# SwiGLU products read back near their use, a lag of three turns, and a ring of eight weight units

## Chip, core and metric

One core of one Trainium2 chip runs the kernel. The metric is the device time of one execution in microseconds (us), lower is better; of several runs the median counts.

## What is computed

A decoder trunk of four layers on 256 tokens of width 1024, all in float32. Each layer is half a SwiGLU feed-forward block, a mixer, and half a second feed-forward block, each behind an RMSNorm and added to x. The mixers of the four layers are a short gated convolution, multi-head latent attention (16 heads, causal), a spatial gating block, and the convolution again.

```python
# x: (1, 256, 1024); D_FF 2816; four layers
def swiglu(x, w_gate, w_up, w_down):
    return (jax.nn.silu(x @ w_gate) * (x @ w_up)) @ w_down
...
    for i in range(DEPTH):
        x = x + 0.5 * swiglu(rms_norm(x, norm_g[i, 0]), ffn_gate[i, 0], ffn_up[i, 0], ffn_down[i, 0])
        hn = rms_norm(x, norm_g[i, 1])
        kind = i % N_MIXERS
        ...
        x = x + mix
        x = x + 0.5 * swiglu(rms_norm(x, norm_g[i, 2]), ffn_gate[i, 1], ffn_up[i, 1], ffn_down[i, 1])
```

The convolution mixer is (b * conv(c * h)) @ w_out with b, c, h parts of x @ w_in. The attention mixer projects to a 416-wide vector (w_a), from it to keys, values (w_ukv) and queries (w_uq), normalises and rotates them, and ends with w_o.

## The kernel before

**Two tiles, one list of weights.** The 256 tokens are two tiles of 128. Each weight matrix is cut into units of 128 x 1024 elements (512 KB), in a fixed order. A unit is loaded from DRAM into one of six raw buffers (`Weights.load`, L93, on SP's queue), split into a high part by ScalarE (`make`, L106) and a low part by VectorE (`complete`, L113), both in a ring of N_UNITS buffers, and used once by tile 0 and once by tile 1. A product of two float32 numbers is three matmuls: high by high, high by low, low by high (`products`, L299, L300, L302). `get` makes units up to AHEAD (4) ahead of tile 0's current one, 3 while a tile is between blocks. The raw buffer of unit u is loaded again, with unit u+6, when the low part of u is written.

**Turns.** Each tile is a Python generator (`stream`); what it issues from one `yield` to the next is a turn, most often one unit, six matmuls of 512 columns. The program is written out by hand: tile 0 gets LAG turns alone (L1004), and then the two take turns, tile 1 first (L1006 to L1009). `later(n, f)` issues f after n turns, those of both tiles counted. All engines execute what is issued to them in that order, and semaphores alone hold them back.

**A feed-forward block.** After IDLE turns without matmuls come 44 turns of gate and up: chunks of 512 columns, where the first three (gate 0, up 0, gate 1) go in two halves of k (`linear_group`). Then 22 turns of down (`rows_into_x`): k-tiles 0 to 9 one by one with 1024 columns, and the last 12 (DOWN_TAIL) in pairs, once for each half of the columns. When a gate chunk is done ScalarE takes Silu of it (L479); when an up chunk is done VectorE makes the product (L487) and transposes it in blocks of 32 (L489) into a `big` buffer. Two chunks make a record (three of them: 8, 8 and 6 k-tiles of 128). `turned` (L269) writes the record to DRAM one turn later (L275), reads it back four turns after the product in four transfers that put the blocks in transposed place (L279), into a second `big`, and from turn 12 on takes it, four k-tiles at a time: ScalarE makes the high part (L285), VectorE the low part (L286), both in slots, of which there are 34. They are held until the down turns use them. There are four `big` buffers and four DRAM buffers for records.

**Around the blocks.** At a block's end x is updated in halves (`residual`, L398 and L400), squared for the norm (L381), and turned for the next block by TensorE (`turn_by_pe`, L261, L441, L253, L254) or through DRAM (L421, L425, L431). The convolution makes c * h (L548), turns it by TensorE three turns later (L261), applies the taps on VectorE (L528, L530) and gates it (L537). In the attention block the streams have turns without matmuls: four ahead of it (IDLE_MLA), three after the queries (Q_WAIT), three ahead of w_o (O_WAIT), and tile 0 has one after each of its four score turns (T0_PACE). L781 ends the rotation of keys and queries, L787 evicts the w_a product, L919 is the exponential, L930 copies the turned probabilities.

Of the kernel before, what the change touches and what calls it, by code (L numbers as in the profile page):

```python
# [24 lines left out]
P = 128  # L25
D = 1024
# [14 lines left out]
PER_RAW = 1  # L41
SMALL = 0
N_UNITS = 9
# [6 lines left out]
LAG = 4  # L50
# [3 lines left out]
SKEW = 2  # L54
# [10 lines left out]

class Weights:


    def __init__(self, nc, raw_pool, pool):
        self.nc, self.raw_pool, self.pool = nc, raw_pool, pool  # L70
        self.raws = []
        self.units = []
# [6 lines left out]
    def add(self, w, c0, width, n_kt, per_unit, k=0):  # L79

        v = w.rearrange("(kt p) n -> p kt n", p=P)
        while k < n_kt:
            n_rows = min(n_kt - k, per_unit * (1 if len(self.units) < SMALL else max(1, PER_RAW * UNIT // (per_unit * width))))
            for j in range(0, n_rows, per_unit):
                self.units.append((len(self.raws), j, min(per_unit, n_rows - j), width))
            self.raws.append((v[:, k : k + n_rows, c0 : c0 + width], n_rows, width))
            k += n_rows

    def load(self, upto):
        while len(self.loaded) < min(upto, len(self.raws)):  # L90
            view, n_rows, width = self.raws[len(self.loaded)]
            raw = self.raw_pool.tile([P, n_rows, width], F32, tag="raw", name=f"raw{len(self.loaded)}")
            self.nc.sync.dma_start(out=raw, in_=view)  # L93
            self.loaded.append(raw)

    def make(self):
        nc = self.nc
        u = len(self.made)
        if u == len(self.units):
            return  # L100
        r, j, n, width = self.units[u]
        self.load(r + 1)
        src = self.loaded[r][:, j : j + n, :]
        hi = self.pool.tile([P, n, width], F32R, tag="whi", name=f"whi{u}")
        lo = self.pool.tile([P, n, width], F32R, tag="wlo", name=f"wlo{u}")
        nc.scalar.activation(hi, src, AF.Copy)  # L106
        self.made.append((hi, lo, n))
        last = u + 1 == len(self.units) or self.units[u + 1][0] > r
        self.half_made.append((hi, lo, src, r + 1 + N_RAW if last else 0))
# [22 lines left out]
def trunk(ctx: ExitStack, tc: tile.TileContext, x, positions, norm_g, ffn_gate, ffn_up, ffn_down,  # L132
          conv_w_in, conv_k, conv_w_out, mla_w_a, mla_q_norm, mla_w_uq, mla_kv_norm, mla_w_ukv,
          mla_q_gain, mla_k_gain, mla_w_o, sg_w_in, sg_v_norm, sg_w_s, sg_b, sg_w_out, out):
    nc = tc.nc

# [7 lines left out]
    banks = ctx.enter_context(tc.tile_pool(name="banks", bufs=8, space=PSUM))  # L144

    ids = [0]
# [38 lines left out]
    W = Weights(nc, raw_pool, w_pool)  # L185
    cursor = [0] * NT
    in_chain = [False] * NT

    def unit(t):
        cursor[t] += 1  # L190
        return W.get(cursor[t] - 1, AHEAD if not any(in_chain) else CHAIN_AHEAD)
# [20 lines left out]
    def start():  # L212
# [7 lines left out]
        make_identity(nc, ident)  # L220
# [83 lines left out]
    def linear(t, a, width, n_kt):  # L304

        ps = acc()
        k = 0
        while k < n_kt:
            w = unit(t)
# [7 lines left out]
    def plan_rows(w, n_kt, tail):  # L317

        W.add(w, 0, D, n_kt - tail, 1)
        for h in range(2):  # L320
            W.add(w, 512 * h, 512, n_kt, 2, n_kt - tail)

    def rows_into_x(t, a, n_kt, tail, factor, then):
# [3 lines left out]
        for k in range(n_kt - tail):  # L327
            products(ps, a(k), k % 4, unit(t), 0, cols, k == 0, False)
            yield
        for h in range(2):  # L330
            for k in range(n_kt - tail, n_kt, 2):
                w = unit(t)
# [12 lines left out]

    def plan_group(parts, width, n_kt):

        for k in range(0, n_kt, n_kt // 2):
            for w, c0 in parts:
                W.add(w, c0, width, k + n_kt // 2, UNIT // width, k)  # L350

    def linear_group(t, a, width, n_kt, done):

        ps = [acc() for _ in done]
        for k0 in range(0, n_kt, n_kt // 2):
            for n in range(len(done)):
                k = k0
                while k < k0 + n_kt // 2:
                    w = unit(t)
                    for j in range(w[2]):  # L360
                        products([ps[n][:, :width]], a[(k + j) // 4], (k + j) % 4, w, j, [slice(0, width)], k + j == 0, k + j == n_kt - 1)
                    k += w[2]
                    if k == n_kt:
                        done[n](ps[n])
                    yield
# [95 lines left out]
    def plan_ffn(i, j):  # L461
        gate, up = ffn_gate[i, j], ffn_up[i, j]
        plan_group([(gate, 0), (up, 0), (gate, 512)], 512, NK)
        W.add(up, 512, 512, NK, 2)
        for c, w in FF_CHUNKS[2:]:
            for m in (gate, up):
                W.add(m, c, w, NK, UNIT // w)
        plan_rows(ffn_down[i, j], DFF // P, DOWN_TAIL)

    def ffn(t, i, j, _, then):  # L470
        a, r = yield from normed(t, IDLE_FIRST if i + j == 0 else (IDLE_DMA, IDLE_PE)[j])
        hs = []
        sg = [None] * len(FF_CHUNKS)
        z = []

# [5 lines left out]
        def up_done(n, ps):  # L481
# [10 lines left out]
            if z[1] == nk:  # L492
                turned(z[0], nk, hs)

        yield from linear_group(t, a, 512, NK, [lambda ps: gate_done(0, ps), lambda ps: up_done(0, ps), lambda ps: gate_done(1, ps)])
        for n, (c, w) in enumerate(FF_CHUNKS):
            if n > 1:
                gate_done(n, (yield from linear(t, a, w, NK)))
                yield
            if n > 0:  # L500
                up_done(n, (yield from linear(t, a, w, NK)))
                yield
        yield from rows_into_x(t, lambda k: hs[k // 4], DFF // P, DOWN_TAIL, 0.5, then)


    def plan_conv(ia):
        plan_group([(conv_w_in[ia], part * D) for part in (1, 2, 0)], 512, NK)
        for part in (1, 2, 0):
            W.add(conv_w_in[ia], part * D + 512, 512, NK, 2)
        plan_rows(conv_w_out[ia], NK, OUT_TAIL)  # L510

    def conv(t, i, ia, shared, then):
# [43 lines left out]
        yield from linear_group(t, a, 512, NK, [lambda ps, f=f: f(0, ps) for f in (c_done, h_done, b_done)])  # L556
        for f in (c_done, h_done, b_done):
            f(1, (yield from linear(t, a, 512, NK)))
# [477 lines left out]
```

## Time and profile before

| | |
|---|---|
| median of 3 runs | 1859.11 us (1858.88 to 1860.58) |
| the profiled execution | 1856.6 us, span 1854.9 us |
| granted TensorE clock, mean | 0.998 |
| TensorE matmul busy | 1833.3 us, 8518 matmuls |
| VectorE, ScalarE busy | 1119.6 us, 913.9 us |
| HBM read and written | 365.67 MB, 33.03 MB |

The span runs from the first to the last instruction. A matmul is pipelined, so the times of single ones overlap, and busy time is the time in which at least one runs. Engines are PE (TensorE matmul), PEld (its weight loads), DVE (VectorE), ACT (ScalarE), POOL (GpSimd) and SP, whose queue issues DMAs. L12 is line 12 of the kernel. "<-" names what an instruction waited for last.

### The profile page before, as it was taken

Reading aid. Unit: us, or ns where it says so; the run is one execution under the profiler, and the core shown is the slowest. Engines: PE = TensorE matmul, PEld = TensorE weight load, DVE = VectorE, ACT = ScalarE, POOL = GpSimd, SP = SyncE. Lnnn points to the kernel's source line nnn. Section 1 sums busy time; section 2 is a strip of 40 time slices with the busy share of each in tenths; the row PEclk is TensorE's granted clock in tenths of the full one; section 3 lists DMA queues with packets and bytes.
Section 4 is the critical chain, followed back from the end, with each engine's and each line's share of the span. In section 5 each row is a group of like instructions: output and inputs, shape, how many; then the busy total and the mean of one; then the engine's idle time right before and its main releaser. Section 6 shows DMA issues by size and latency. Waiting matters only on the chain.

```text
span 1854.9 us, 23375 instructions
## 1 busy us (share of the span) xinstructions
PE 1833.3 (99%) x8518; PEld 1506.0 (81%) x8518; DVE 1119.6 (60%) x1357; ACT 913.9 (49%) x1300; POOL 103.9 (6%) x222
## 2 busy tenths in 40 slices
PE   8999999999999989999999999999999999999999
PEld 6888878888888878888888888888888888788887
DVE  5655676655665576666556555665645665775662
ACT  5443645443644376544454446554545454545451
POOL 1000000000501031000010001000000000000000
PEclk9999999999999999999999999999999999999999
DMA  7776657776777550687777766577857785657782
GB/s 265 241 240 218 209 179 216 240 241 210 235 244 238 193 160 15 201 259 232 221 238 256 228 220 216 175 232 234 264 185 243 242 261 178 213 181 235 233 269 75
DMA packets 228980, 400.26 MB, mean 216 GB/s; under 512 B 17126, under 2 KB 77696, under 8 KB 228864
## 3 DMA queue, kind: packets, MB, share of 16 engines
q1 hardware_dynamic: 227856, 397.08, 67.0%
q8 instruction: 66, 1.08, 0.2%
q0 software_dynamic: 608, 1.11, 0.2%
q10 hardware_dynamic: 400, 0.57, 0.1%
q14 instruction: 50, 0.41, 0.1%
HBM read 365.67 MB, written 33.03 MB: 215 GB/s over the span
## 4 chain that ended last, share of the span: by engine, by line
PE 96%; ACT 2%; DVE 2%; issue 0%; DMA 0%; DVEq 0%; ACTq 0%
PE acc L299 31%; PE acc L300 31%; PE acc L302 31%; PE tr L261 1%; PE acc L938 1%; PE acc L911 1%; ACT whi L106 1%; DVE wlo L113 0%; DVE s L530 0%; ACT s L836 0%; ACT s L253 0%; PE acc L620 0%; DMA s<-in_norm_g_dram 0%; ACT s L817 0%; ACT s L860 0%
## 5 line engine op out<-in xcount | busy, mean ns | idle before, releaser
L299 PE MATMUL acc<-whi,s 128*128 128x512 f32 (+1 forms) x2664 | 1025.2, 385 | 2.8 <-ACT whi L106 1.3
L300 PE MATMUL acc<-wlo,s 128*128 128x512 f32 (+1 forms) x2664 | 1019.8, 383 | 2.1 <-DVE wlo L113 2.1
L302 PE MATMUL acc<-whi,s 128*128 128x512 f32 (+1 forms) x2664 | 988.2, 383 | 0.0
L113 DVE TENSOR_TENSOR wlo<-raw,whi 128x1024 fp32r<-128x1024 f32 (+1 forms) x634 | 747.3, 1212 | 131.0 <-ACT whi L106 129.2
L106 ACT ACTIVATE whi<-raw 128x1024 fp32r<-128x1024 f32 (+1 forms) x634 | 636.6, 1047 | 138.9 <-PE acc L302 120.3
L299 PEld LDWEIGHTS acc<-whi,s 128*128 128x128 f32 x2664 | 500.9, 188 | 107.8 <-ACT whi L106 2.5
L300 PEld LDWEIGHTS acc<-wlo,s 128*128 128x128 f32 x2664 | 501.0, 188 | 106.0 <-DVE wlo L113 3.0
L302 PEld LDWEIGHTS acc<-whi,s 128*128 128x128 f32 x2664 | 500.7, 188 | 106.1 <-DVE s L254 0.7
L479 ACT ACTIVATE s<-acc,rstd 128x512 f32<-128x512 f32 (+1 forms) x96 | 62.6, 652 | 446.4 <-PE acc L302 440.4
L487 DVE SCALAR_TENSOR_TENSOR s<-acc,rstd,s 128x512 f32<-128x512 f32 (+1 forms) x96 | 67.7, 705 | 173.6 <-PE acc L302 171.8
L286 DVE TENSOR_TENSOR s<-big,s 128x512 fp32r<-128x512 f32 x96 | 61.8, 644 | 128.1 <-ACT s L285 127.9
L381 ACT ACTIVATE s<-x 128x512 bf16<-128x512 f32 x48 | 30.2, 630 | 163.6 <-DVE x L400 125.9
L254 DVE TENSOR_TENSOR s<-s,s 128x512 fp32r<-128x512 f32 (+1 forms) x58 | 39.9, 688 | 107.6 <-ACT s L253 107.6
L389 POOL TENSOR_TENSOR total<-ss,ss 128x1 f32<-128x1 f32 x26 | 14.8, 570 | 1417.1 <-ACT s L381 1417.1
L400 DVE SCALAR_TENSOR_TENSOR x<-acc,x 128x512 f32<-128x512 f32 x32 | 22.1, 692 | 117.3 <-PE acc L302 117.2
L285 ACT ACTIVATE s<-big 128x512 fp32r<-128x512 f32 x96 | 56.3, 586 | 22.1 <-DMA big<-turn 22.0
L489 DVE STREAM_TRANSPOSE big<-s 128x512 f32<-128x512 f32 (+1 forms) x96 | 64.1, 667 | 3.3
L253 ACT ACTIVATE s<-s 128x512 fp32r<-128x512 f32 (+1 forms) x58 | 36.5, 629 | 42.1 <-DVE s L537 21.6
L431 ACT ACTIVATE s<-s,columns 128x128 f32<-128x128 f32 x136 | 43.1, 388 | 1.9 <-DMA s<-xturn 1.7
L261 PE MATMUL tr<-ident,s 128*128 128x128 f32 (+1 forms) x222 | 33.3, 276 | 9.8 <-DVE s L781 5.1
L261 PEld LDWEIGHTS tr<-ident,s 128*128 128x128 f32 (+1 forms) x222 | 25.8, 138 | 17.9 <-DVE s L781 7.3
L415 DVE STREAM_TRANSPOSE s<-x 128x512 f32<-128x512 f32 x34 | 24.2, 711 | 1.2
(123 smaller groups left out, 410.6 us busy)
## 6 DMA issues: line engine op xcount, KB each, us to landing
raw<-in_ffn_gate_dram SPq DMA_DIRECT2D x176, 512.0 KB, 4.8
raw<-in_ffn_up_dram SPq DMA_DIRECT2D x176, 512.0 KB, 5.0
raw<-in_ffn_down_dram SPq DMA_DIRECT2D x176, 512.0 KB, 5.0
raw<-in_conv_w_in_dram SPq DMA_DIRECT2D x48, 512.0 KB, 4.7
turn<-big SPq DMA_DIRECT2D x32, 512.0 KB, 4.0
big<-turn SPq DMA_DIRECT2D x128, 128.0 KB, 4.4
xturn<-s SPq DMA_DIRECT2D x34, 256.0 KB, 4.2
s<-xturn SPq DMA_DIRECT2D x136, 64.0 KB, 2.0
```

The source lines that it names most:

```text
L106: nc.scalar.activation(hi, src, AF.Copy)
L113: self.nc.vector.tensor_tensor(out=lo, in0=src, in1=hi.bitcast(F32), op=ALU.subtract)
L261: nc.tensor.transpose(tr[: part.shape[-1], n, :], part, ident)
L285: nc.scalar.activation(hi.rearrange("p k (i b) -> p k i b", b=32), src, AF.Copy)
L286: nc.vector.tensor_tensor(out=lo.rearrange("p k (i b) -> p k i b", b=32), in0=src, in1=hi.bitcast(F32).rearrange("p k (i b) -> p k i b", b ...
L299: nc.tensor.matmul(ps, lhsT=ah[:, k, :], rhs=wh[:, wk, c], start=first, stop=False)
L300: nc.tensor.matmul(ps, lhsT=ah[:, k, :], rhs=wl[:, wk, c], start=False, stop=False)
L302: nc.tensor.matmul(ps, lhsT=al[:, k, :], rhs=wh[:, wk, c], start=False, stop=last)
L431: nc.scalar.activation(xg[:, k, :].rearrange("p (i b) -> p i b", b=32), y[:, :, k], AF.Copy, scale=g[:, k : k + 1])
L479: nc.scalar.activation(sg[n], ps[:, :w], AF.Silu, scale=r)
L487: nc.vector.scalar_tensor_tensor(out=h, in0=ps[:, :w], scalar=r, in1=sg[n], op0=ALU.mult, op1=ALU.mult)
L489: nc.vector.transpose(z[0][:, :, k0 : k0 + w // P].rearrange("p j k b -> p k j b"), h.rearrange("p (k j b) -> p k j b", j=4, b=32))
```

## The change

The weights are no longer planned by functions of their own: the whole program is first run without an engine (`Blank`), and the order of first use of the keys (matrix, k, n, column, width, copy) is the order of the units. `linear` and `linear_group` now share their loop. `turned` becomes a class whose parts are called by the feed-forward block: the write as before one turn after the product, the read H_READ (7) and the take H_TAKE (2) of the tile's own turns ahead of the turn that first uses the k-tiles. LAG goes from 4 to 3, N_UNITS from 9 to 8. `own` and `pause`, lists of zeros, are read and never set.

```diff
 UNIT = 1024
-PER_RAW = 1
-SMALL = 0
-N_UNITS = 9
+N_UNITS = 8
 N_RAW = 6
 N_SLOTS = 34
 N_BIG = 4
 N_DRAM = 4
 AHEAD = 4
 CHAIN_AHEAD = 3
-LAG = 4
+LAG = 3
+H_READ, H_TAKE = 7, 2
 DOWN_TAIL, OUT_TAIL = 12, 4
 X_TURN, X_WRITE, X_READ, X_TAKE = 2, 1, 3, 12
...
-    def get(self, u, ahead):
+    def get(self, key, ahead):
+        if self.rehearsed:
+            if key not in self.index:
+                self.index[key] = len(self.order)
+                self.order.append(key)
+            return Blank(), Blank(), key[2]
+        u = self.index[key]
         for _ in range(2):
-            if len(self.made) < min(len(self.units), u + ahead):
+            if len(self.made) < min(len(self.order), u + ahead):
                 self.make()
         return self.made[u]
...
-    def turned(z, n, parts):
-
-        d = dram.tile([4, 32, 4, n, 32], F32, tag="turn", name=name("turn"))
-        y = big([P, 4, n, 32])
-
-        def write():
-            nc.sync.dma_start(out=d.rearrange("i a j k b -> (i a) j k b"), in_=z)
-
-        def read():
+    class Turned:
+
+
+        def __init__(self, z, n):
+            self.n = n
+            self.d = dram.tile([4, 32, 4, n, 32], F32, tag="turn", name=name("turn"))
+            later(1, lambda: nc.sync.dma_start(out=self.d.rearrange("i a j k b -> (i a) j k b"), in_=z))
+
+        def read(self):
+            self.y = big([P, 4, self.n, 32])
             for j in range(4):
-                nc.sync.dma_start(out=y[32 * j : 32 * j + 32], in_=d[:, :, j].rearrange("i a k b -> a i k b"))
-
-        def take(k):
-            m = min(4, n - k)
+                nc.sync.dma_start(out=self.y[32 * j : 32 * j + 32], in_=self.d[:, :, j].rearrange("i a k b -> a i k b"))
+
+        def take(self, k):
+            m = min(4, self.n - k)
             hi, lo = slot([P, m, P], F32R), slot([P, m, P], F32R)
-            src = y[:, :, k : k + m].rearrange("p i k b -> p k i b")
+            src = self.y[:, :, k : k + m].rearrange("p i k b -> p k i b")
             nc.scalar.activation(hi.rearrange("p k (i b) -> p k i b", b=32), src, AF.Copy)
             nc.vector.tensor_tensor(out=lo.rearrange("p k (i b) -> p k i b", b=32), in0=src,
                                     in1=hi.bitcast(F32).rearrange("p k (i b) -> p k i b", b=32), op=ALU.subtract)
-            parts.append((hi, lo))
-
-        later(1, write)
-        later(4, read)
-        for k in range(0, n, 4):
-            later(12 + k, lambda k=k: take(k))
+            return hi, lo
...
+    def linear_group(t, a, parts, width, n_kt):
+
+        ps = [acc() for _ in parts]
+        for k0 in range(0, n_kt, n_kt // 2):
+            for n, (m, c0, done) in enumerate(parts):
+                yield from linear(t, a, m, c0, width, n_kt, ps[n], k0, k0 + n_kt // 2)
+                if k0:
+                    done(ps[n])
+                    yield
...
-                turned(z[0], nk, hs)
-
-        yield from linear_group(t, a, 512, NK, [lambda ps: gate_done(0, ps), lambda ps: up_done(0, ps), lambda ps: gate_done(1, ps)])
-        for n, (c, w) in enumerate(FF_CHUNKS):
-            if n > 1:
-                gate_done(n, (yield from linear(t, a, w, NK)))
-                yield
-            if n > 0:
-                up_done(n, (yield from linear(t, a, w, NK)))
-                yield
-        yield from rows_into_x(t, lambda k: hs[k // 4], DFF // P, DOWN_TAIL, 0.5, then)
-
-
-    def plan_conv(ia):
-        plan_group([(conv_w_in[ia], part * D) for part in (1, 2, 0)], 512, NK)
-        for part in (1, 2, 0):
-            W.add(conv_w_in[ia], part * D + 512, 512, NK, 2)
-        plan_rows(conv_w_out[ia], NK, OUT_TAIL)
+                recs.append(Turned(z[0], nk))
...
+        def take(n):
+            hs[n] = recs[n // 2].take(n % 2 * 4)
+
+        events = {}
+        for n in range(len(FF_CHUNKS)):
+            k = 4 * n
+            at = DFF // 64 + (k if k < DFF // P - DOWN_TAIL else DFF // P - DOWN_TAIL + (k - DFF // P + DOWN_TAIL) // 2)
+            if n % 2 == 0:
+                events.setdefault(at - H_READ, []).append(lambda n=n: recs[n // 2].read())
+            events.setdefault(at - H_TAKE, []).append(lambda n=n: take(n))
+        for at, _ in enumerate(body()):
+            for event in events.get(at, ()):
+                event()
+            yield
...
+    start()
+    streams = [stream(t) for t in range(NT)]
+    live = [True] * NT
+
+    def advance(t):
+        W.complete()
+        live[t] = next(streams[t], "end") != "end"
+        turn[0] += 1
+        run_due()
+
+    for _ in range(LAG):
+        advance(0)
+    while any(live):
+        for t in reversed(range(NT)):
+            if pause[t]:
+                pause[t] -= 1
+            elif live[t]:
+                advance(t)
```

The plan functions (`plan_group`, `plan_rows`, `plan_ffn` and the like) are removed, and each call of `linear`, `rows_into_x` and `unit` names its matrix and place instead.

## Rows read from the trace of the kernel before

**Rows 1.** Page, busy time of each engine (share of the span) and instructions.
```profile
PE 1833.3 (99%) x8518; PEld 1506.0 (81%) x8518; DVE 1119.6 (60%) x1357; ACT 913.9 (49%) x1300; POOL 103.9 (6%) x222
```

**Rows 2.** Stretches: us; busy PE, PEld, DVE, ACT, POOL; clock, DMA share, GB/s.
```profile
0.00:20.00 20.00, 14.99 (x60) 10.39 (x61) 11.21 (x15) 10.82 (x16) 7.03 (x19) 1.00 0.91 333
...
222.00:242.00 20.00, 19.09 (x90) 15.34 (x89) 16.73 (x36) 10.69 (x15) 0.00 (x0) 1.00 0.47 149
...
684.00:692.00 8.00, 6.59 (x41) 5.39 (x42) 7.62 (x24) 7.87 (x15) 4.31 (x5) 1.00 0.46 130
...
708.00:716.00 8.00, 6.78 (x37) 5.93 (x38) 2.16 (x5) 4.88 (x20) 0.00 (x0) 0.79 0.00 0
...
750.00:1150.00 400.00, 400.00 (x1830) 328.65 (x1829) 234.99 (x249) 195.64 (x266) 14.84 (x24) 1.00 0.72 229
...
1850.00:1855.00 5.00, 0.95 (x5) 0.43 (x3) 0.69 (x1) 0.00 (x0) 0.00 (x0) 1.00 0.14 52
```

**Rows 3.** Who TensorE waited for, whole span: us, times, longest us.
```profile
PE tr L261 <- DVE s L781: 5.1, 6, 2.2
PE acc L300 <- DVE wlo L113: 2.1, 3, 0.8
PE tr L261 <- DVE s L548: 1.8, 2, 0.9
...
PE tr L261 <- ACT s L919: 1.0, 1, 1.0
PE acc L938 <- DVE s L930: 0.8, 1, 0.8
```

**Rows 4.** Stretches of 50 us, columns as in rows 2.
```profile
50.00:100.00 50.00, 50.00 (x217) 40.23 (x216) 30.35 (x34) 24.71 (x29) 0.00 (x0) 1.00 0.74 235
...
1300.00:1350.00 50.00, 50.00 (x264) 42.59 (x263) 32.38 (x37) 25.55 (x32) 0.00 (x0) 1.00 0.82 267
```

**Rows 5.** Page, groups of instructions: busy us, mean ns, idle before and releaser.
```profile
L113 DVE TENSOR_TENSOR wlo<-raw,whi 128x1024 fp32r<-128x1024 f32 (+1 forms) x634 | 747.3, 1212 | 131.0 <-ACT whi L106 129.2
L106 ACT ACTIVATE whi<-raw 128x1024 fp32r<-128x1024 f32 (+1 forms) x634 | 636.6, 1047 | 138.9 <-PE acc L302 120.3
...
L487 DVE SCALAR_TENSOR_TENSOR s<-acc,rstd,s 128x512 f32<-128x512 f32 (+1 forms) x96 | 67.7, 705 | 173.6 <-PE acc L302 171.8
L286 DVE TENSOR_TENSOR s<-big,s 128x512 fp32r<-128x512 f32 x96 | 61.8, 644 | 128.1 <-ACT s L285 127.9
...
L285 ACT ACTIVATE s<-big 128x512 fp32r<-128x512 f32 x96 | 56.3, 586 | 22.1 <-DMA big<-turn 22.0
L489 DVE STREAM_TRANSPOSE big<-s 128x512 f32<-128x512 f32 (+1 forms) x96 | 64.1, 667 | 3.3
```

**Rows 6.** DMA: a raw load (KB, us to landing); landing of the turned records.
```profile
raw<-in_ffn_down_dram SPq DMA_DIRECT2D x176, 512.0 KB, 5.0
...
DMA to landing us min/median/max: 2.0/3.9/7.9
```

**Rows 7.** Who SP's queue waited for, whole span: us, times, longest us.
```profile
SPq L93 <- DVE wlo L113: 810.1, 407, 43.5
...
SPq L279 <- DMA turn<-big: 82.1, 34, 4.5
```

**Rows 8.** Timeline, VectorE, convolution of layer 0: start us, us, instruction, count.
```profile
226.12 0.74 DVE L530 SCALAR_TENSOR_TENSOR s<-s,columns,s 128x128 f32<-128x128 f32 x2
...
229.05 0.68 DVE L537 TENSOR_TENSOR s<-tr,s 128x512 f32<-128x512 f32 x1
...
232.52 0.75 DVE L548 SCALAR_TENSOR_TENSOR s<-acc,rstd,s 128x512 f32<-128x512 f32 x1
```

**Rows 9.** Timeline, start of the kernel, VectorE and TensorE.
```profile
12.91 3.50 DVE L113 TENSOR_TENSOR wlo<-raw,whi 128x1024 fp32r<-128x1024 f32 x3 [0.26 <-ACT whi L106]
...
13.91 0.60 PE L261 MATMUL tr<-ident,x 128*128 128x128 f32 x4
...
17.73 0.50 PE L299 MATMUL acc<-whi,s 128*128 128x512 f32 x1
```

More of the change, by code (lines that the diff above doesn't have):

```diff
@@ L63, with __getattr__, __call__, __getitem__ @@
 FF_CHUNKS = [(c, min(512, DFF - c)) for c in range(0, DFF, 512)]
-class Weights:
[L69 to L72, printed above, removed]
+class Blank:
+    def __getattr__(self, _):
+        return self
+    def __call__(self, *_, **__):
+        return self
+    def __getitem__(self, _):
+        return self
+class Weights:
+    def __init__(self, nc, raw_pool, pool, matrices, order):
+        self.nc, self.raw_pool, self.pool, self.matrices = nc, raw_pool, pool, matrices
+        self.rehearsed = order is None
+        self.order = order or []
+        self.index = {key: n for n, key in enumerate(self.order)}
         self.made = []
@@ L77, in __init__ @@
         self.wanted = 0
[L79 to L87, printed above, removed]
     def load(self, upto):
-        while len(self.loaded) < min(upto, len(self.raws)):
-            view, n_rows, width = self.raws[len(self.loaded)]
-            raw = self.raw_pool.tile([P, n_rows, width], F32, tag="raw", name=f"raw{len(self.loaded)}")
+        while len(self.loaded) < min(upto, len(self.order)):
+            m, k, n, c0, width, _ = self.order[len(self.loaded)]
+            view = self.matrices[m[0]][m[1:]].rearrange("(kt p) n -> p kt n", p=P)[:, k : k + n, c0 : c0 + width]
+            raw = self.raw_pool.tile([P, n, width], F32, tag="raw", name=f"raw{len(self.loaded)}")
             self.nc.sync.dma_start(out=raw, in_=view)
@@ L183, in run_due, with unit @@
             p[2]()
-    W = Weights(nc, raw_pool, w_pool)
-    cursor = [0] * NT
+    W = Weights(nc, raw_pool, w_pool, {
+        "gate": ffn_gate, "up": ffn_up, "down": ffn_down, "conv_in": conv_w_in, "conv_out": conv_w_out, "w_a": mla_w_a,
+        "w_ukv": mla_w_ukv, "w_uq": mla_w_uq, "w_o": mla_w_o, "sg_in": sg_w_in, "sg_out": sg_w_out}, order)
     in_chain = [False] * NT
-    def unit(t):
-        cursor[t] += 1
-        return W.get(cursor[t] - 1, AHEAD if not any(in_chain) else CHAIN_AHEAD)
+    pause = [0] * NT
+    own = [0] * NT
+    def unit(t, m, k, n, c0, width):
+        copy = 0
+        if own[t]:
+            own[t] -= 1
+            copy = 1
+        return W.get((m, k, n, c0, width, copy), AHEAD if not any(in_chain) else CHAIN_AHEAD)
     xs = [fixed([P, D], f"x{t}") for t in range(NT)]
@@ L302, in products, with linear @@
             nc.tensor.matmul(ps, lhsT=al[:, k, :], rhs=wh[:, wk, c], start=False, stop=last)
[L304 to L309, printed above, removed]
+    def linear(t, a, m, c0, width, n_kt, ps=None, k0=0, k1=None):
+        ps = ps or acc()
+        k = k0
+        while k < (k1 or n_kt):
+            w = unit(t, m, k, UNIT // width, c0, width)
             for j in range(w[2]):
@@ L315, in linear, with rows_into_x @@
         return ps
[L317 to L323, printed above, removed]
+    def linear_group(t, a, parts, width, n_kt):
[6 more added lines that the diff above has]
+                    yield
+    def rows_into_x(t, a, m, n_kt, tail, factor, then):
         ps = [acc(), acc()]
@@ L458, in normed @@
         return Lhs(t), factor(sums_of_x[t])
[L461 to L468, printed above, removed]
     def ffn(t, i, j, _, then):
         a, r = yield from normed(t, IDLE_FIRST if i + j == 0 else (IDLE_DMA, IDLE_PE)[j])
-        hs = []
+        gate, up, down = (("gate", i, j), ("up", i, j), ("down", i, j))
+        hs = [None] * len(FF_CHUNKS)
         sg = [None] * len(FF_CHUNKS)
         z = []
+        recs = []
         def gate_done(n, ps):
@@ L968, in trunk @@
         counts[kind] += 1
-    for kind, i, j in blocks:
-        plan = kinds[kind][0]
-        plan(i, j) if kind == "ffn" else plan(j)
     shareds = [{} for _ in blocks]
@@ L990, in stream @@
                     then = (next_i, 1, (True, next_kind != "mla"))
-            yield from kinds[kind][1](t, i, j, shareds[n], then)
-    with tc.manual_schedule(engines=MANUAL):
-        start()
-        streams = [stream(t) for t in range(NT)]
-        live = [True] * NT
-        def advance(t):
-            W.complete()
-            live[t] = next(streams[t], "end") != "end"
-            turn[0] += 1
-            run_due()
-        for _ in range(LAG):
-            advance(0)
-        while any(live):
-            for t in reversed(range(NT)):
-                if live[t]:
-                    advance(t)
-        while put_off:
-            turn[0] += 1
-            run_due()
+            yield from kinds[kind][0](t, i, j, shareds[n], then)
+    start()
[14 more added lines that the diff above has]
+                advance(t)
+    while put_off:
+        turn[0] += 1
+        run_due()
+    return W.order
 _INS = ["x", "positions", "norm_g", "ffn_gate", "ffn_up", "ffn_down", "conv_w_in", "conv_k", "conv_w_out",
```

101 lines of the change are left out of this document (46 added, 55 removed).

## The prediction

> **What bounds the kernel now.** I read three views in this order. First the busy time of the engines: TensorE is busy for 1833.3 of 1854.9 us [rows 1], so 21.6 us of its time are idle. Then the same sum by stretches, to see where those 21.6 us lie [rows 2]: 20.00 - 14.99 = 5.0 us in the first 20 us, 0.9 us in 222 to 242 us, as much near 1608 us (the two waits for L548 [rows 3]), 4.1 us in the last 5 us, which makes 10.9, and the other 10.7 us lie in the attention block between 660 and 716 us (two of its stretches are shown). Everywhere else, in all eight feed-forward blocks after the start, the busy time equals the length of the stretch, as 400.00 of 400 from 750 us on. Third, who was waited for [rows 3]: the list of TensorE holds no wait for a take (L285, L286) or for the turned product. The pace of such a stretch is 217 matmuls in 50 us [rows 4], 230 ns for one of 512 columns, so a turn (one weight unit, six such matmuls) is 1.38 us and a pair of turns (one of each tile) 2.77 us.
>
> So the feed-forward blocks, where most of the diff works, have nothing to give: a faster transfer, a freer slot or an earlier product there ends no wait of TensorE. They can only lose. What can be won lies in at most 5.0 + 10.7 + 1.8 us, and it is the lag that reaches it.
>
> The Trainium skill (Perfetto Trace Analysis, section Identifying the Most-Contended Engine) holds matmul busy time to be a poor measure of headroom and wants the busy share of LDWEIGHTS instead, which is 81% here [rows 1]. By that one might hope for far more than 1%. The constant 217 matmuls in 50 us [rows 4] speaks against it here; by the one the gain is capped at some 1% of the span, by the other not.
>
> **The change part by part.** Times are made against the profiled execution, 1856.6 us (span 1854.9 and 1.7 around it). It lies 2.5 us under the median of the runs, 1859.1; I add these 2.5 at the end.
>
> *Order of the weights, rewritten planning.* The order list now comes from a rehearsal by first use. Tile 0 leads tile 1 by three turns throughout, and both idle the same number of turns, so first use is the order that the plan functions gave; shapes of loads and units are the same. Cost 0. `copy`, `own` and `pause` stay 0.
>
> *Ring of eight, lag three.* When tile 0 makes unit u+3 (AHEAD 4), tile 1 has just used u-3 instead of u-4. Then five older units are live in eight buffers, where six were in nine: three free buffers before and after. Cost 0; it would cost something only if ScalarE's weight casts waited longer for a buffer, and they are due 3 pairs = 8.3 us ahead.
>
> *Reads moved.* The four reads of a turned record leave their place four turns of the program after the product and go seven own turns ahead of use: body turns 37, 45 and 50, use at 44, 52 and 57. That concentrates 2 x (512 + 512 + 384) KB of reads and 2 x 384 KB of writes in 16 pairs (44 us): 3.7 MB in 44 us, 83 GB/s, on top of a 512 KB unit per 2.77 us, 189 GB/s; 272 together. The stretch at 1300 us moved 267 GB/s with TensorE never idle, and the start moved 333 [rows 2, 4]. So it fits. On SP's queue a read is 4 issues, and behind it stand only raw weight loads. A raw load is issued when its ring place is free (810 us of SP's waits are that [rows 7]); six units of 2.77 us, less cast 1.05, subtraction 1.21 and landing 5.0 [rows 5, 6], leave 9 us before ScalarE misses it. One read a block finds no free big buffer but the one whose write has just been issued: record 1 of tile 0, at body turn 45, behind the write of record 2 (body turn 43). It holds SP for at most that write's landing, 3.9 us in the middle and 7.9 at most [rows 6]; the 9 us cover it. In return the reads that now wait for their own write (82.1 us of SP's time in 34 waits [rows 7]) find it long landed. Cost 0.
>
> *Takes moved.* A take is 0.59 us of ScalarE and 0.64 of VectorE, 96 of each [rows 5], not more than before. They go from the gate and up turns to two own turns before use. From read to use lie 14 turns of the program, 19.4 us; worst landing of the write plus worst landing of the read plus the take are 7.9 + 7.9 + 1.2 = 17.0. From take to use lie three turns, 4.1 us, against 1.2 us for itself and, ahead of it in the queues, one weight cast (1.05) on ScalarE or a product, its transpose and one subtraction on VectorE (0.71 + 0.67 + 1.21) [rows 5]. 1.2 + 2.6 = 3.8 is just under 4.1 even with all of that starting late; and both engines run ahead of TensorE in the down turns. Load there: ScalarE 1.05 + 12 x 0.59 / 16 = 1.5 us of each pair's 2.77, VectorE 1.21 + 12 x 0.64 / 16 = 1.7. Cost 0; if the cover is gone, see the second rival. Slots are held for less time; since TensorE waited for none, the gain is 0.
>
> The Trainium skill (DMA: Bandwidth & Descriptors, section Rules for kernel authors) speaks against this part: issue a transfer early and wait late. By that rule the change gives cover away and would be slower; the landing of 3.9 us against 13.8 us from read to take [rows 6] says that enough is left.
>
> *Lag three in the convolution blocks.* The idle 0.9 us at 232 and at 1608 us is tile 1's transposes waiting for its product L548 [rows 3]. In the rows [rows 8] VectorE does tile 0's taps until 226.8, two subtractions, tile 0's gating (229.05) and more subtractions, and only then L548 at 232.5. With lag three tile 1's turn comes two program turns earlier, before tile 0's gating is queued: VectorE has one subtraction between the taps and L548, so it is done at 226.8 + 1.2 + 0.7 = 228.7, and the transposes stand three turns after the end of tile 1's part, near 230. Both waits go: -1.8 (bounds -1.8 and +0.9).
>
> *Lag three at the start.* Tile 0's units 0 and 1 wait for casts as before. But tile 1's first turn now comes after two turns of tile 0 more instead of three, and wants its left operand, made by L441, L253, L254 behind subtraction 3 on VectorE: ready at 12.91 + 2 x 1.2 (subtractions 2 and 3 [rows 9]) + 0.69 + 0.6, near 16.5, where TensorE, which ends unit 1 at 13.9 [rows 9] and then has four transposes (0.4) and unit 2 (1.38) to do, arrives at 15.7. The present wait at 17.7 [rows 9] becomes some 0.8 us. +0.4 (bounds -0.6 and +1.5).
>
> *Lag three in the attention block.* (a) Entry: tile 0's four idle turns were covered by four turns of tile 1, now by three; tile 1's transposes then wait for its residual, +1.0 (0 to 1.4), while the 0.6 us wait for a subtraction at 665 us (part of L300's 2.1 [rows 3]) finds it done: -0.6. (b) Between 684 and 692 us ScalarE is busy 7.87 of 8 us [rows 2]: it is the bound there, and one linear turn of tile 1 less (1.1 us of TensorE) lies inside: +1.1. (c) Front of the softmax: of the pairs in which neither tile has matmuls two become one, and tile 1's first scores come before tile 0's first probabilities are wanted; the waits for L919 and L930, 1.0 and 0.8 us [rows 3], shrink: -1.5. The granted clock is 0.79 in 708 to 716 us [rows 2], a mean of its two levels 2.4 and 1.2 GHz, where TensorE had just been idle: 0.21 x 8 = 1.7 us lost, which may go or come again. Sum 0.0 (bounds -5.8, with both low-clock stretches gone, and +3.5).
>
> Sum: -1.8 + 0.4 + 0.0 = -1.4; 1856.6 - 1.4 = 1855.2, against the median 1857.7 us.
>
> **The rivals.** *Faster through the attention block.* The lag suits its queues: both low-clock stretches and the waits for L919 and L930 vanish, -5, with the convolution's -1.8: 1852 to 1854 us. For it: 5.1 us of waits for L781 are queue order [rows 3], and order is what a lag changes. Against it: ScalarE is full there, whatever the order. *Slower through late takes.* In the turns where gate and up end, ScalarE's and VectorE's queues are held by results of TensorE, so a take two turns before use can come late, with a weight cast queued behind it; it decides from the point where take plus queue exceeds 4.1 us, that is 0.3 us over my 3.8. At 0.5 to 1 us in each of 16 (block, tile) cases it is +8 to +16: 1866 to 1874 us. For it: the sum is tight on VectorE; against it: the takes of before also stand behind casts, and cost TensorE nothing. *Slower through the attention block*: (a) and (b) in full, (c) none, another low-clock stretch: about +4.5, 1862 to 1864. *The change doesn't do what it says*: the later read changes nothing since all of it is hidden, and only the lag acts; that is my forecast.
>
> **How the numbers follow.** Runs agree within some 0.1%, and 0.2% (3.7 us) is about what a measurement can tell from no change. Forecast (1855.4 to 1862.8): 0.62. Faster rival: 0.21. Late takes: 0.11, the attention block slower: 0.06, together 0.17. The range leaves out the far end of the faster rival and most of the late takes: 1852 to 1866 us.
>
> **What would show it.** Right: TensorE's busy time within 1 us of 1833, no wait for L548 in the list, waits for takes absent, stretches of the feed-forward blocks still 50.00 of 50. Wrong: waits of L299 or L302 for the take's cast or subtraction, once a block; a busy time that grows; ScalarE waiting for big<-turn more than the present 22 us [rows 5]; more than two low-clock stretches.

## The result, and the profile after

The changed kernel takes 1872.1 us (median of 5 runs, 1866.08 to 1875.15), against 1858.88 us (5 runs, 1857.05 to 1860.58) for the kernel before on the same chip: ratio 1.0069, 95% interval 1.0049 to 1.0089. It is slower by 13 us, where 1857.7 us and no change were forecast, with 1852 to 1866 as the range.

Line numbers have moved: the products are now L317, L318 and L320, transposes by TensorE L283, a weight's high part L107 and low part L113, left operands L275 and L276, the residual L401 (after a mixer) and L403 (after a feed-forward block), the product of the convolution L555, the rotation L778, the takes L308 and L309.

The page of the changed kernel: busy time of each engine, to be held against [rows 1].

```profile
span 1870.0 us, 23382 instructions
PE 1838.4 (98%) x8518; PEld 1508.3 (81%) x8518; DVE 1122.9 (60%) x1357; ACT 919.8 (49%) x1300; POOL 95.8 (5%) x222
```

The span grew by 15.1 us. TensorE's idle time went from 21.6 to 1870.0 - 1838.4 = 31.6 us, +10.0, and its busy time by 5.1. Who TensorE waited for (total us, times, longest us), against [rows 3]:

```profile
PE tr L283 <- DVE x L401: 7.4, 4, 1.9
PE tr L283 <- DVE s L778: 6.6, 7, 1.5
PE acc L317 <- ACT s L275: 2.9, 2, 2.2
PE tr L283 <- DVE s L555: 1.9, 4, 0.7
PE tr L283 <- DVE x L403: 1.8, 1, 1.8
PE tr L283 <- ACT s L916: 1.8, 1, 1.8
...
PE acc L318 <- DVE wlo L113: 1.5, 2, 0.8
```

No take stands in it. At the top is a wait that the kernel before didn't have: transposes of x for the residual of a mixer, once after each of the four mixers, and once more ahead of the attention block (L403). Together they are 9.2 us, against 10.0 that the idle time grew by; the other waits rose and fell by up to 1.6 us each and nearly cancel. By stretches (columns as in rows 2):

```profile
20.00:230.00 210.00, 210.00 (x958) 172.09 (x957) 123.92 (x141) 103.34 (x136) 3.67 (x9) 1.00 0.72 226
...
288.00:291.00 3.00, 1.16 (x8) 0.67 (x7) 2.51 (x4) 1.14 (x3) 1.81 (x3) 1.00 0.76 253
291.00:662.00 371.00, 371.00 (x1697) 304.46 (x1696) 217.18 (x230) 177.98 (x240) 37.18 (x108) 1.00 0.73 228
662.00:665.00 3.00, 1.18 (x8) 0.74 (x7) 1.29 (x2) 1.61 (x5) 0.00 (x0) 1.00 0.22 81
665.00:724.00 59.00, 47.55 (x266) 40.87 (x266) 41.37 (x119) 46.22 (x107) 21.02 (x29) 0.91 0.27 88
...
768.00:1209.00 441.00, 441.00 (x2027) 362.04 (x2026) 260.46 (x277) 220.77 (x302) 12.27 (x27) 1.00 0.72 225
...
1674.00:1682.00 8.00, 6.15 (x22) 4.64 (x21) 5.45 (x7) 3.03 (x6) 1.81 (x3) 0.79 0.59 168
```

The feed-forward blocks are still full to the last us (210.00 of 210, 371.00 of 371, 441.00 of 441). Each new hole is a short one at the end of a block: 1.8 us of 288 to 291, 1.8 of 662 to 665. One of them is followed by TensorE's lower clock level, 1.2 GHz: mean 0.79 over the 8 us from 1674.

The first hole in the timeline of the changed kernel (start us, us, engine, instruction, idle before and releaser):

```profile
287.40 0.69 DVE L401 TENSOR_TENSOR x<-acc,x 128x512 f32<-128x512 f32 x1 [0.60 <-PE acc L320]
...
288.13 0.71 DVE L418 STREAM_TRANSPOSE s<-x 128x512 f32<-128x512 f32 x1
...
288.36 0.40 PE L320 MATMUL acc<-whi,s 128*128 128x512 f32 x1
...
288.76 1.18 DVE L113 TENSOR_TENSOR wlo<-raw,whi 128x1024 fp32r<-128x1024 f32 x1
...
289.87 0.68 DVE L401 TENSOR_TENSOR x<-acc,x 128x512 f32<-128x512 f32 x1
...
290.60 0.66 PE L283 MATMUL tr<-ident,x 128*128 128x128 f32 x4 [1.84 <-DVE x L401]
```

TensorE ends tile 1's last matmul of the half at 288.76. VectorE first does a weight's low part, then the residual, which ends at 290.55, and the transposes are the very next thing in TensorE's program. In the kernel before, its residual L398 of the same half ran at 288.22 to 288.91 while TensorE had a turn of tile 0 until 289.41, and the transposes followed without a gap:

```profile
288.22 0.69 DVE L398 TENSOR_TENSOR x<-acc,x 128x512 f32<-128x512 f32 x1 [0.22 <-PE acc L302]
...
289.18 0.39 PE L302 MATMUL acc<-whi,s 128*128 128x512 f32 x1
...
289.41 0.60 PE L261 MATMUL tr<-ident,x 128*128 128x128 f32 x4
```

Why the lag does that can be counted in the program. A tile's last turns in a mixer are E-3 and E-2 for the first half of x, whose residual is issued in E-2, then E-1 and E. IDLE 2 is one empty turn, E+1, since the first `yield` of it only ends turn E; matmuls begin again in E+2. X_TURN 2 issues the transposes after one more turn of the program, which is tile 0's: with lag L it is tile 0's E-2+L. With lag 4 that is E+2, a full turn. With lag 3 it is E+1, the empty one. With lag 2 it is E, full again. Ahead of the attention block TensorE turns the second half of x, whose residual is issued in E; tile 0's turn behind it is E+L, and with IDLE_MLA 4 the turns E+1 to E+3 are empty: full with lag 4, empty with 3 and with 2. That is theory A. Theory B is the rival of late takes, theory C that a smaller lag simply leaves less cover.

The lag does a second thing there. Tile 0's turn ahead of tile 1's E-2 is E-3+L: the empty E+1 with lag 4, but E with lag 3, which gives VectorE the residual of tile 0's second half (287.40), its turning (L418) and a weight's low part right ahead of tile 1's residual. So that residual, whose matmuls end at 288.76, starts 1.1 us later; with lag 4 it starts as soon as they end. Of the hole's 1.84 us, 1.1 are VectorE's queue and 0.7 the residual itself. The other three holes show the same order on VectorE.

### The profile page after: what moved, and what is told of

It is laid out like the page before. It is cut to its first block, busy times and chain, and to the rows that moved or that the text cites. A ratio compares the mean times of both kernels' runs of the same rounds, so it can differ in the third digit from the quotient of the medians.

```text
span 1870.0 us, 23382 instructions
## 1 busy us (share of the span) xinstructions
PE 1838.4 (98%) x8518; PEld 1508.3 (81%) x8518; DVE 1122.9 (60%) x1357; ACT 919.8 (49%) x1300; POOL 95.8 (5%) x222
## 4 chain that ended last, share of the span: by engine, by line
PE 94%; DVE 3%; ACT 2%; issue 1%; DMA 0%; POOL 0%; DVEq 0%; ACTq 0%
PE acc L317 31%; PE acc L320 30%; PE acc L318 30%; PE tr L283 1%; DVE wlo L113 1%; PE acc L908 1%; PE acc L935 1%; DVE s L537 1%; ACT whi L107 0%; DVE x L401 0%; DVE s L535 0%; ACT s L833 0%; ACT s L275 0%; PE acc L624 0%; DMA s<-in_norm_g_dram 0%
## 5 line engine op out<-in xcount | busy, mean ns | idle before, releaser
L317 PE MATMUL acc<-whi,s 128*128 128x512 f32 (+1 forms) x2664 | 1025.3, 385 | 3.8 <-ACT s L275 2.9
L318 PE MATMUL acc<-wlo,s 128*128 128x512 f32 (+1 forms) x2664 | 1020.3, 383 | 1.5 <-DVE wlo L113 1.5
L320 PE MATMUL acc<-whi,s 128*128 128x512 f32 (+1 forms) x2664 | 989.1, 383 | 0.0
L113 DVE TENSOR_TENSOR wlo<-raw,whi 128x1024 fp32r<-128x1024 f32 (+1 forms) x634 | 749.0, 1212 | 282.7 <-ACT whi L107 277.9
L107 ACT ACTIVATE whi<-raw 128x1024 fp32r<-128x1024 f32 (+1 forms) x634 | 640.9, 1049 | 185.3 <-PE acc L320 155.8
L317 PEld LDWEIGHTS acc<-whi,s 128*128 128x128 f32 x2664 | 500.8, 188 | 108.7 <-ACT s L275 4.3
L320 PEld LDWEIGHTS acc<-whi,s 128*128 128x128 f32 x2664 | 500.9, 188 | 106.7 <-DVE s L276 1.0
L318 PEld LDWEIGHTS acc<-wlo,s 128*128 128x128 f32 x2664 | 501.1, 188 | 105.7 <-DVE wlo L113 2.3
L309 DVE TENSOR_TENSOR s<-big,s 128x512 fp32r<-128x512 f32 x96 | 61.2, 638 | 50.4 <-ACT s L308 48.4
L403 DVE SCALAR_TENSOR_TENSOR x<-acc,x 128x512 f32<-128x512 f32 x32 | 22.1, 690 | 104.1 <-PE acc L320 104.1
L276 DVE TENSOR_TENSOR s<-s,s 128x512 fp32r<-128x512 f32 (+1 forms) x58 | 39.9, 688 | 73.1 <-ACT s L275 73.1
L308 ACT ACTIVATE s<-big 128x512 fp32r<-128x512 f32 x96 | 54.7, 582 | 16.5 <-DMA big<-turn 16.5
L275 ACT ACTIVATE s<-s 128x512 fp32r<-128x512 f32 (+1 forms) x58 | 36.5, 629 | 50.6 <-DVE s L544 28.6
L283 PE MATMUL tr<-ident,s 128*128 128x128 f32 (+1 forms) x222 | 34.2, 281 | 11.0 <-DVE s L778 6.6
L283 PEld LDWEIGHTS tr<-ident,s 128*128 128x128 f32 (+1 forms) x222 | 26.1, 139 | 19.6 <-DVE s L778 9.1
L418 DVE STREAM_TRANSPOSE s<-x 128x512 f32<-128x512 f32 x34 | 24.2, 712 | 1.2
```

The costliest lines, as they stand in the source:

```text
L107: self.nc.scalar.activation(hi, self.loaded[u], AF.Copy)
L113: self.nc.vector.tensor_tensor(out=lo, in0=src, in1=hi.bitcast(F32), op=ALU.subtract)
L283: nc.tensor.transpose(tr[: part.shape[-1], n, :], part, ident)
L308: nc.scalar.activation(hi.rearrange("p k (i b) -> p k i b", b=32), src, AF.Copy)
L309: nc.vector.tensor_tensor(out=lo.rearrange("p k (i b) -> p k i b", b=32), in0=src, in1=hi.bitcast(F32).rearrange("p k (i b) -> p k i b", b ...
L317: nc.tensor.matmul(ps, lhsT=ah[:, k, :], rhs=wh[:, wk, c], start=first, stop=False)
```

## Experiments

### Each half of the change alone: lag4_ring9 and before_lag3

```diff
# lag4_ring9: the changed kernel
-N_UNITS = 8
+N_UNITS = 9
-LAG = 3
+LAG = 4
# before_lag3: the kernel before
-N_UNITS = 9
+N_UNITS = 8
-LAG = 4
+LAG = 3
```

> The changed kernel with LAG 4 and N_UNITS 9, so that only the late reads and takes (and the rehearsed order) are left of the change. Theory A (the lag puts tile 0's empty turn between tile 1's residual and its transposes): the five waits for L401 and L403, 9.2 us in the changed kernel, are gone, and the time is that of the kernel before, ratio 0.998 to 1.002, 1856 to 1862 us. Theory B (the late reads and takes cost the time): it stays near 1872 us, ratio 1.005 or more.

> The kernel before with LAG 3 and N_UNITS 8 alone; products read back and taken early as before. Theory A: all of the loss is here, ratio 1.005 to 1.009, 1867 to 1875 us, with four waits for L398 of 1.8 to 1.9 us after the mixers and one for L400 of 1.8 us ahead of the attention block. Theory B: within 0.2% of the kernel before.

lag4_ring9: 1859.16 us, ratio 1.0001 (0.9992 to 1.0010). before_lag3: 1871.71 us, ratio 1.0068 (1.0051 to 1.0085). lag4_ring9's list of TensorE's waits has none for L401 or L403. The late reads and takes cost nothing that can be told, and the lag, with the ring of eight, costs all of it. TensorE's waits in before_lag3, whose lines are those of the kernel before:

```profile
PE tr L261 <- DVE x L398: 7.4, 4, 1.9
PE tr L261 <- DVE s L781: 6.2, 7, 1.5
PE acc L299 <- ACT s L253: 3.0, 2, 2.3
PE tr L261 <- DVE x L400: 1.8, 1, 1.8
```

The waits for the two residuals are those of the changed kernel to a tenth, with the product turned early; L781 and L253 differ by up to 0.4 us. The late reads cost nothing here (1.0001): TensorE never waited for a take. The Trainium skill (DMA: Bandwidth & Descriptors, section Rules for kernel authors) advises issuing a transfer early and waiting for it late. The prediction weighed that as a reason for a loss; none came here, where the landing was covered.

### The ring alone: lag4_ring8

```diff
# the changed kernel
-LAG = 3
+LAG = 4
```

> The changed kernel with LAG 4 and its ring of eight weight units, one buffer fewer than lag and look-ahead were set up for (nine). Theory A (the lag alone cost the time, the ring nothing): as with nine, 1856 to 1863 us, no wait of L317 or L318 for L107 or L113 beyond the 3.1 us of the run with nine. Rival (the ring is short): ScalarE's casts wait for tile 1's use of a unit and come late, waits for L107 and L113 of some 0.5 us each appear in the feed-forward blocks, 1865 us or more.

1859.95 us, ratio 1.0009 (1.0000 to 1.0018). TensorE's waits for L107 and L113 are 0.9 and 1.8 us, not more than with nine. One buffer fewer costs at most 0.2%, and no wait shows it.

### Less lag still: lag2

```diff
# the changed kernel
-LAG = 3
+LAG = 2
```

> The changed kernel with LAG 2, ring of eight as it is. Theory A: tile 0's empty turn then falls one pair earlier or later against tile 1's residual, a turn of tile 0 with matmuls stands before the transposes, and the four waits for L401 after the mixers are gone, although the lag is smaller; the attention block may lose more. Time 1860 to 1875 us. Theory C (the smaller the lag, the less cover): the waits for L401 grow beyond 1.9 us each or are more than four, and the time is 1878 us or more.

1880.3 us, ratio 1.0117 (1.0099 to 1.0136). TensorE's waits:

```profile
PE tr L283 <- DVE s L555: 9.3, 4, 2.3
...
PE tr L283 <- ACT s L560: 4.2, 2, 2.9
PE tr L283 <- DVE x L403: 3.2, 1, 3.2
...
PE tr L283 <- DVE x L401: 0.2, 1, 0.2
```

The waits after the mixers, 7.4 us with lag 3, are 0.2 us with lag 2. So it is the pairing, not the amount of cover, that made them. The time is longer than I allowed for all the same, and lies where theory C put it: the convolution now has 13.5 us of waits (L555, L560) where lag 3 has 1.9, and the one ahead of the attention block grows, where tile 0's turn E+2 is empty. Theory C is wrong for the wait in question and right for others.

### Giving the transposes their cover back: xturn3 and xturn4

```diff
# the changed kernel; xturn4 has 4 in the same place
-X_TURN, X_WRITE, X_READ, X_TAKE = 2, 1, 3, 12
+X_TURN, X_WRITE, X_READ, X_TAKE = 3, 1, 3, 12
```

> The changed kernel with X_TURN 3 instead of 2: the transposes of x by TensorE are issued one turn of the program later, so that a turn of tile 1 with six matmuls (1.38 us) stands between its residual and its transposes after the mixers. Theory A: the four waits for L401 (7.4 us) fall to 2 us or less together, the one for L403 ahead of the attention block stays (only empty turns follow there), and the time falls by 5 to 8 us against the changed kernel, to 1863 to 1868 us. Theory C (a lag of three leaves too little cover, wherever the transposes stand): the wait moves to the consumers of the transposes (L317, L320 for L275, L276) and the time stays near 1872 us.

> The changed kernel (LAG 3) with X_TURN 4: the transposes of x by TensorE two turns of the program later than there. After the mixers a turn of each tile with matmuls then stands between tile 1's residual and its transposes, and ahead of the attention block tile 0's first linear turn does. Theory A: the waits for L401 (7.4 us, 3.2 with X_TURN 3) and for L403 (1.8) are gone; 1861 to 1865 us, what is left being the attention block and the start. Theory C (the lag leaves too little cover): the waits come back at the consumers of the transposes, for L275 and L276, and the time is 1866 us or more.

xturn3: 1865.99 us, ratio 1.0042 (1.0027 to 1.0056); the waits for L401 are 3.2 us in 4 instead of 7.4, above the 2 that I expected. What is left is VectorE's queue: the timeline has tile 1's turn in front of the transposes until 290.9, and the residual, whose matmuls ended at 289.5, starts only at 290.96, behind tile 0's residual, L418 and L113.

```profile
289.86 1.18 DVE L113 TENSOR_TENSOR wlo<-raw,whi 128x1024 fp32r<-128x1024 f32 x1
...
290.49 0.40 PE L320 MATMUL acc<-whi,s 128*128 128x512 f32 x1
290.96 0.68 DVE L401 TENSOR_TENSOR x<-acc,x 128x512 f32<-128x512 f32 x1
...
291.70 0.66 PE L283 MATMUL tr<-ident,x 128*128 128x128 f32 x4 [0.81 <-DVE x L401]
```

xturn4: 1860.68 us, ratio 1.0017 (1.0007 to 1.0026); no wait for L401 is left. With the lag at three, some 10 of the 13 us are back, by the ratios, through two program turns for one kind of transposes. The waits did not move to L275 or L276 (2.9 us as before), which is against theory C.

The wait for L403 ahead of the attention block stayed, against the expectation: 2.1 us, although a turn of tile 0 now stands in front of the transposes. In xturn4's timeline:

```profile
662.93 0.69 DVE L276 TENSOR_TENSOR s<-s,s 128x512 fp32r<-128x512 f32 x1 [1.14 <-ACT s L275]
663.54 0.68 DVE L403 SCALAR_TENSOR_TENSOR x<-acc,x 128x512 f32<-128x512 f32 x1
...
664.27 0.86 PE L283 MATMUL tr<-ident,x 128*128 128x128 f32 x4 [2.08 <-DVE x L403]
```

Tile 1's residual L403 stands in VectorE's queue behind the low part (L276) of a half that came through DRAM, and that one waits 1.14 us for ScalarE. The expectation below calls it tile 0's half. It is tile 1's own first half: tile 0's was taken at 650.6, and with X_TAKE 12 the take of tile 1's is issued just ahead of tile 1's turn E.

### Taking that half later: xturn4_xtake14

```diff
# the changed kernel
-X_TURN, X_WRITE, X_READ, X_TAKE = 2, 1, 3, 12
+X_TURN, X_WRITE, X_READ, X_TAKE = 4, 1, 3, 14
```

> LAG 3 with X_TURN 4 and X_TAKE 14 instead of 12: the halves of x that go through DRAM are also taken two program turns later. In the run with X_TURN 4 the wait for L403 ahead of the attention block stayed (2.1 us), although a turn of tile 0 stood between: VectorE did the low part of tile 0's half (L276, behind ScalarE's L434) ahead of tile 1's residual L403. Theory A': that order is the cause; with the take behind the residual the wait for L403 falls under 1 us and ScalarE's waits for xturn (24.0 us) fall under 12 us; time 1857 to 1861 us. Rival: the residual is late for another reason, the wait stays at 1.8 us or more.

1886.04 us, ratio 1.0151 (1.0137 to 1.0165). TensorE's waits:

```profile
PE acc L317 <- ACT s L275: 15.7, 17, 3.4
...
PE tr L283 <- DVE x L403: 0.9, 1, 0.9
```

The wait for L403 fell from 2.1 to 0.9 us, so the queue order was the cause of 1.2 us of it; in the 0.9 the residual still stands behind another L276, that of tile 0's second half. The time was missed by far: the takes now have only one turn of each tile between them and their use at the block ends, and TensorE waits for L275 17 times. A cut of two program turns in that cover costs 25 us. The waits are only part of it: against xturn4's profile TensorE's idle time grew by 13.6 us (24.5 to 38.1) and its time at 1.2 GHz from 3.4 to some 20 us, about half of which is lost. I had looked at the wait to be mended and not at the use behind it.

### Where late takes begin to cost: take1

```diff
# lag4_ring9
-H_READ, H_TAKE = 7, 2
+H_READ, H_TAKE = 7, 1
```

> The changed kernel with LAG 4, N_UNITS 9 and H_TAKE 1: takes one own turn ahead of use, so that one turn of the program (1.38 us) stands between take and use instead of three (4.1 us). The sum in the prediction (1.2 us for the take, 2.6 us of queue ahead of it, 3.8 together) taken as it stands: waits of TensorE for L308 and L309 of up to 2.4 us in the 16 cases at the end of gate and up, and less in the others, +16 to +40 us. Rival (ScalarE and VectorE run ahead of TensorE by more than a turn in the down turns, and the queue has long been worked off): waits for L308 and L309 of under 3 us together, 1857 to 1863 us.

1862.99 us, ratio 1.0024 (1.0015 to 1.0034), at the upper end of the rival's range. The list of TensorE's matmuls that wait shows none for L308 or L309. The list of its weight loads does, seven times, and the timeline has it once in a feed-forward block in seven of them, where the matmul that wants the low part starts some 0.40 us after the one ahead of it instead of 0.23:

```profile
PEld acc L320 <- DVE s L309: 3.0, 7, 0.4
```

```profile
177.41 0.68 DVE L309 TENSOR_TENSOR s<-big,s 128x512 fp32r<-128x512 f32 x1
...
177.73 0.40 PE L318 MATMUL acc<-wlo,s 128*128 128x512 f32 x1
...
178.14 0.50 PE L320 MATMUL acc<-whi,s 128*128 128x512 f32 x1
```

With that and the slower matmul behind it, it is 0.27 us each, 1.9 us in all; the other 2.5 us that the ratio stands for (4.4) I can't place. So the point from which late takes decide lies about one own turn under H_TAKE 2. My 3.8 us for take and queue would have made it 2.4 us each: the engines run ahead of TensorE, and the queue was worked off.

### More lag, and other places for transposes: lag5, lag5_q5, lag5_q5_k4, lag4_c4_q5

```diff
# lag5: the changed kernel
-LAG = 3
+LAG = 5
-N_UNITS = 8
+N_UNITS = 10
-N_SLOTS = 34
+N_SLOTS = 30
# lag5_q5: that and Q_TURN 3 -> 5; lag5_q5_k4: that and K_TURN 2 -> 4
# lag4_c4_q5: LAG 4, N_UNITS 9, Q_TURN 5, and
-            later(3, lambda: convolved(j, z))
+            later(4, lambda: convolved(j, z))
```

> The changed kernel with LAG 5, N_UNITS 10 and N_SLOTS 30 (slots that the late takes leave free pay for the two units). Theory A: no empty turn of tile 0 falls behind tile 1's residual, so no waits for L401 or L403; the attention block has one more turn of tile 1 to cover tile 0's start and no other pairing that is known to be bad: 1855 to 1861 us. Rival: any lag but the one for which the turn counts were set makes new waits, as LAG 2 did in the convolution (L555, L560): 1864 us or more.

> LAG 5, N_UNITS 10, N_SLOTS 30 and Q_TURN 5 instead of 3: the transposes of the queries two program turns later, so that TensorE doesn't stand in front of them while ScalarE and VectorE are at the rotation (L778, 8.7 us with LAG 5). If order is the cause of that wait, it falls under 4 us, and the time to 1852 to 1857 us, below the kernel before. If ScalarE is the bound of that stretch, whatever the order, TensorE waits elsewhere for the same time: 1857 to 1862 us.

> The late reads and takes with LAG 4 and N_UNITS 9, the transposes of the convolution's product one program turn later (4 instead of 3) and Q_TURN 5. The two waits for L555 (1.8 us) go; of the waits for L778 (5.1 us) as much as order, not ScalarE's load, makes. If all: 1852 to 1856 us. If the load is the bound in the attention block: 1856 to 1859 us, the waits for L778 coming back as others.

> As the run with LAG 5 and Q_TURN 5, with K_TURN 4 instead of 2: the transposes of the keys two program turns later too. TensorE's waits for L850 (5.9 us there) fall under 3 us if order makes them, and the time goes to 1851 to 1855 us. If ScalarE's load is the bound of the stretch, the waits come back elsewhere and the time stays at 1855 to 1857 us.

| kernel | us | ratio to the kernel before | waits in the attention block and convolution |
|---|---|---|---|
| lag5 | 1859.78 | 1.0006 (0.9996 to 1.0015) | L778 8.7, L555 none |
| lag5_q5 | 1855.53 | 0.9981 (0.9972 to 0.9990) | L778 1.1, L850 5.9 |
| lag5_q5_k4 | 1855.40 | 0.9981 (0.9972 to 0.9990) | L778 5.2, L850 none |
| lag4_c4_q5 | 1856.40 | 0.9987 (0.9979 to 0.9996) | L778 0.6, L850 3.6, L555 0.2 |

Lag 5 has no wait for L401, L403 or L555, as theory A has it. The slots that the late takes leave free pay for its two extra units. The queries' transposes two turns later bring it under the kernel before by 0.19%, about what can be told from no change, with an interval that leaves out 1. In TensorE's list of lag5_q5 the wait moved from L778 to the keys:

```profile
PE tr L283 <- DVE s L850: 5.9, 3, 3.4
...
PE tr L283 <- DVE s L778: 1.1, 1, 1.1
```

and when the keys are moved too it goes back to L778, the time staying. So of the attention block's wait only some 2 us went away by order, and the rest moved, as the second branch of those expectations says; only lag5_q5's time, 1855.53, is that of the first. That ScalarE's load bounds the rest is argued from its 7.87 of 8 us [rows 2] and not shown: no run made that load smaller. lag4_c4_q5 removed the convolution's wait and most of L778's, and gained 0.13%; what each of its two edits gave was not measured alone.

## Why the prediction was wrong

**What bounds the kernel** held: TensorE is full in the feed-forward blocks before and after, and idle in the start, the convolution, the attention block and the last few us. The idle block ends are new. The share of weight loads was 81% before and after, and no run gained more than 0.2%, within the cap of some 1% that the prediction set.

**Order, ring, reads, takes** were put at 0, and lag4_ring9 (1.0001) and lag4_ring8 (1.0009) measured 0 to 0.1%. The write's wait on SP's queue went as said: reads waiting for their own write fell from 82.1 us [rows 7] to 1.5. In its place reads wait 42.3 us for raw loads of the down weights, and ScalarE's wait for the records went from 22.0 [rows 5] to 16.5 us. From the changed kernel's list for SP's queue:

```profile
SPq L302 <- DMA raw<-in_ffn_down_dram: 42.3, 24, 2.9
...
SPq L302 <- DMA turn<-big: 1.5, 2, 0.9
```

The longest landing of a record was 11.0 us, where the prediction's sum had 7.9 twice; with 11.0 twice that sum is 23.2, over the 19.4 us from read to use. So its margin was less safe than it looked, though TensorE waited for none. The rival of late takes is refuted at H_TAKE 2, with about a turn to spare.

**Lag three** is the step that failed, and by leaving something out. The prediction went through the start, the convolution and the attention block and put every other block end at nothing, without a reason. Its one sentence that touches them, on the order of the weights, is that "both idle the same number of turns". That says that the two tiles keep their distance; it doesn't say what of tile 0 stands between tile 1's residual and its transposes, or ahead of that residual on VectorE. Four block ends at 1.8 to 1.9 us, 7.4 together, were not in the sum. The mechanism was in it once, at the entry of the attention block: "tile 1's transposes then wait for its residual, +1.0". That wait came, at 1.8 us, above its bound of 1.4; of the 2.1 us that it has in xturn4, xturn4_xtake14 puts 1.2 on VectorE's queue. I didn't ask where else the same code runs.

**Its other terms.** Convolution, -1.8: the two waits fell from 0.9 us to some 0.2, but two new ones of 0.7 came in the second halves, which the sum had not looked at; 1.8 became 1.9, zero in effect. Start, +0.4: TensorE's busy time in the first 20 us fell from 14.99 [rows 2] to 14.86, so +0.1. Attention block, 0.0 with bounds -5.8 and +3.5: its waits grew from some 10.1 to 13.0 us, of which L403 is +1.8 and L778 +1.5, and its time at the lower clock from 6.8 to 10.2 us in the profiled runs, half of which is lost, +1.7; +4.6, above the upper bound. Part (c), -1.5, came to nothing: L916, the same wait as L919, rose from 1.0 to 1.8 us, and the 0.8 us for L930 went.

**The sum as measured**: 7.4 after the mixers, 0.1 convolution, 0.1 start, 4.6 attention block, 1.7 for the lower clock at 1674 (0.21 x 8), 13.9 of the span's 15.1 us. The rest, 1.2 us, I can't place. The two terms for the lower clock, 3.4 together, are those of one profiled execution and differ from one to the next.

**The forecast of which rival**: slower was given 0.17, by two other mechanisms. The late takes didn't cost. The slower attention block, given 0.06 at +4.5, came at about its size (4.6), though its waits are in part others than it named. The omitted term alone gives 1857.7 + 7.4 = 1865.1, just inside the range; with the attention block's 4.6 it is 1869.7, past 1866. The faster rival counted 5.1 us of waits for L781 as queue order; lag5_q5 and lag5_q5_k4 show that most of it moves to other waits.

## What to carry to other kernels

When a hand-ordered program of two streams gets another distance between them, list every pair "produced by a slow engine, consumed by the bound engine n turns later" and write out which turn of the other stream fills those n turns at the new distance: an empty turn there leaves the whole latency uncovered, and whether it falls there isn't monotone in the distance (0.2, 7.4 and 0 us for lags 2, 3 and 4). Write out too what stands ahead of the producer on its own engine: it made 1.1 of the 1.84 us here. A mechanism found at one place of a loop is to be multiplied by the places where that code runs. Before a consumer is moved to win a wait, its own use must be covered too (X_TAKE 14 cost 25 us for 1.2).

## What the hardware showed beside that

A wait of 1.9 us was followed by the lower clock once in four like cases: the three after 288, 765 and 1209 us show a granted clock of 1.00 in the 8 us behind them, the one at 1674 us a mean of 0.79 over 8 us. In the attention block, with work that is nearly the same, the time at the lower level differed from profile to profile; lag5's profile has

```profile
680.00:730.00 50.00, 40.07 (x218) 36.41 (x217) 31.07 (x92) 34.54 (x84) 14.02 (x15) 0.76 0.13 43
```

(mean clock 0.76 over 50 us, 24 us at 1.2 GHz), and lag5_q5's had 10 us of it there. Such differences of several us between single profiles are why the verdicts above rest on the medians.
